# A hybrid mixer layer on one core: the four tiles of the normalised input begin 32, 64, 160 and 192 bytes off the weights' place, mod 256

## The chip, the core and the metric

The kernel runs on one core of a Trainium2 chip. The metric is the device time of one execution in microseconds (us); of several runs the median counts. Engines are named as the profile names them: PE is TensorE (matmuls), PEld its weight loads, DVE is VectorE, ACT ScalarE, POOL GpSimd and SP the engine that issues most transfers. SBUF is the on-chip memory of 128 partitions from which TensorE reads both operands; a tile has the same address in each partition. "Place" means below: the first byte of an operand in its partition, mod 256.

## What is computed

One layer of a decoder trunk over 512 tokens of width 1024, in float32:

```
u = rms_norm(h, norm_mix_pre);  proj = u @ w_in           # 1024 -> 10 slots of 256, 4 gates of 1024
y_a..y_d = four token mixers of the slots                 # width 256 each
branch_out[k] = y_k @ w_branch[k]
merged = sum_k sigmoid(gate_k) * branch_out[k]
h = h + rms_norm(merged @ w_out, norm_mix_post)
u = rms_norm(h, norm_mlp_pre)
h = h + rms_norm(square(relu(u @ w_up)) @ w_down, norm_mlp_post)
```

## The kernel before

TensorE works on float32r operands. To keep float32's precision each operand is split into a high and a low part (hi, lo), and each product is made of three matmuls in `mm3` (lines 238 to 240): hi x hi, hi x lo, lo x hi. Every matmul has a weight load of its own (its first operand, 128 x 128, 512 bytes per partition) and streams its second operand, nearly always 512 columns, 2048 bytes per partition.

The input, multiplied by the gain of the norm, stands transposed in four tiles: `uh[0]`, `uh[1]` (high parts) and `ul[0]`, `ul[1]` (low parts), each 128 x 4 x 512; tile 0 has the contraction steps k = 0 to 3, tile 1 k = 4 to 7. `U(uh, k)` picks 512 columns of it. They are filled at the start (`xhi`, `xlo`, lines 264 to 271) and used until the last gate:

- L323: the first two slots, 96 matmuls, interleaved with the arrival of the data;
- `slot_mm`: the other slots but one and all gates, by `mm3`, weights from `whi` and `wlo`, streams from `uh` and `ul`, into banks `mm` or `sm`. Of three matmuls the first streams uh with whi, the second (L239) ul with whi, the third (L240) uh with wlo, as the profile names them;
- the slot c_i, where the roles are exchanged: pieces of `uh` and `ul` are the weights and 256 columns of the w tiles are streamed (96 matmuls, named `mm<-whi,uh` and the like).

In between stand small float32 matmuls of the mixers (L612, L698, L721 and others), two matmuls that spread the norm's factors over the partitions (L369 and L370, streams from a tile named t, weights a tile of ones) and the branch projections (streams `yhi`, `ylo`).

Behind them come the output projection, its norm, and the MLP. The MLP's input takes the same four buffers of pool `up` again, as `u2h` and `u2l`; the results of its up part stand in banks `ub`, those of its down part in `db`.

Places: a pool lays its buffers one behind the other. All pools that hold matmul operands of 512 columns have buffers whose size is a multiple of 256 bytes, but the pool of tiles named t, whose buffers are of 4224 bytes. So in the program before the weights and the streams `uh`, `ul`, `u2h`, `u2l`, `yhi`, `ylo` all have place 0, and the buffers of t have place 0 and 128 by turns; the one that L369 and L370 stream has 128.

Which instruction stands where on an engine is set by the order in the code and by a scheduler; the order is the same in both programs.

Of the kernel before, what the change touches and what calls it, by code (L numbers as in the profile page):

```python
# [9 lines left out]
F32R = mybir.dt.float32r  # L10
# [5 lines left out]
P = 128  # L16
T = 512
# [32 lines left out]
def tile_hybrid_trunk(ctx: ExitStack, tc: tile.TileContext, x0, xT, xn, wts, dn, par, bd, cst, msk, gains, out):  # L50
# [4 lines left out]
    up = ctx.enter_context(tc.tile_pool(name="up", bufs=4))  # L55
# [17 lines left out]
    def nm(s):  # L73
        cnt[0] += 1
        return f"{s}_{cnt[0]}"
# [90 lines left out]
    def split(hi, lo, src, pin=False):  # L166
        a_ = act.activation(hi, src, AF.Copy)  # L167
        d_ = dve.tensor_tensor(lo, src, hi.bitcast(F32), ALU.subtract)  # L168
        if pin:
            K(a_)  # L170
            K(d_)
# [79 lines left out]
            dve.tensor_tensor(t, t, h, ALU.mult)  # L251
            dve.scalar_tensor_tensor(y, t, 1.5, y, ALU.add, ALU.mult)

    uh = [up.tile([P, 4, T], F32R, tag="u", name=nm("uh")) for _ in range(2)]
    ul = [up.tile([P, 4, T], F32R, tag="u", name=nm("ul")) for _ in range(2)]

    def U(lst, k, a=0, b=T):
        return lst[k // 4][:, k % 4, a:b]
# [180 lines left out]
    o, _ = PAR["corr"]  # L439
# [387 lines left out]
    for ku in range(4):  # L827
        wh, wl = unit()
        for kk in range(2):
            k = 2 * ku + kk  # L830
# [71 lines left out]
    u2h = [None, None]  # L902
    u2l = [None, None]
# [9 lines left out]

    def put(t, j, tv):
        if u2h[j] is None:
            u2h[j] = up.tile([P, 4, T], F32R, tag="u", name=nm("u2h"))
            u2l[j] = up.tile([P, 4, T], F32R, tag="u", name=nm("u2l"))
        split(u2h[j][:, :, t * P : t * P + P], u2l[j][:, :, t * P : t * P + P], tv)

    for t in range(NT):  # L920
# [5 lines left out]
    for j in range(2):  # L926
        put(0, j, tb0[j])

    def mid():
        tb1 = trans(1, mm_bank)  # L930
        for j in range(2):
            put(1, j, tb1[j])
# [53 lines left out]
    for h in range(2):  # L986
        for s in range(2):
            us[s, h] = unit()
            up_mm(bks[s], us[s, h], h, 0, 256)
            if (s, h) in ((1, 0), (0, 1)):  # L990
                t = 2 if h == 0 else 3
                tb = dn_bank()
                for k in range(NK):
                    pe.transpose(tb[:, k // 4, (k % 4) * P : (k % 4) * P + P], u2[t][:, k * P : k * P + P], ident)
                for j in range(2):
                    put(t, j, tb[:, j].rearrange("p (k t) -> p k t", k=4))
# [267 lines left out]
```

## Time and profile before

| | |
|---|---|
| time, median of 3 runs | 748.35 us (748.03 to 748.45) |
| the profiled execution's own time | 748.08 us |
| its span, first to last instruction | 746.3 us |
| PE busy | 735.8 us (99%), 3506 records |
| PEld busy | 620.0 us (83%) |
| DVE, ACT, POOL busy | 535.6 (72%), 312.9 (42%), 6.8 us (1%) |
| TensorE's granted clock, mean | 0.997 of full speed |

A matmul's record is longer than the distance to the next matmul's start, since matmuls are pipelined; records therefore overlap, and busy time is their union. A weight load's record lies beside the matmul before its own. The chain of waits, unlike the records, gives each matmul only the time until the next.

### The profile page before, as it was taken

To read this page: it belongs to the slowest core of one execution; us is meant where nothing else is said; L and a number is where in the kernel's file an instruction comes from. 1 tells how busy PE (TensorE), PEld (TensorE's weight loads), DVE (VectorE), ACT (ScalarE), POOL (GpSimd) and SP (SyncE) were. 2 spreads that over 40 slices of the span, in tenths; PEclk is the share of its full clock that TensorE was granted. 3 is DMA by queue.
4 is the path that set the end of the run, shared out by engine and by line. 5 is a ranking of instruction groups with operands and counts; after the bars stand their busy time and mean duration, and the time that the engine had idled before them with its cause. 6 is when DMAs were issued, how large, how long until landed. Compare 5 with 4: busy or idle time off the path is not lost.

```text
span 746.3 us, 8881 instructions
## 1 busy us (share of the span) xinstructions
PE 735.8 (99%) x3506; PEld 620.0 (83%) x3506; DVE 535.6 (72%) x776; ACT 312.9 (42%) x404; POOL 6.8 (1%) x11
## 2 busy tenths in 40 slices
PE   9999999999999999999999999999999999999995
PEld 7888988888888888888888988888888888888884
DVE  6798347559997476654748785787879685977786
ACT  6434122336324322332444575644445452636232
POOL 1100000000000000000000000000000000000000
PEclk9999999999999999999999999999999999999998
DMA  9634232222222253323332705042423324040312
GB/s 326 244 117 138 96 101 88 83 85 85 94 82 79 85 217 105 102 85 112 113 113 87 296 15 187 38 149 77 141 84 113 113 78 148 0 141 29 132 66 85
DMA packets 22761, 84.59 MB, mean 113 GB/s; under 512 B 2624, under 2 KB 3520, under 8 KB 20928
## 3 DMA queue, kind: packets, MB, share of 16 engines
q1 hardware_dynamic: 22288, 83.74, 32.7%
q8 instruction: 27, 0.44, 0.2%
q10 hardware_dynamic: 432, 0.29, 0.1%
q14 instruction: 14, 0.11, 0.1%
HBM read 79.83 MB, written 4.19 MB: 113 GB/s over the span
## 4 chain that ended last, share of the span: by engine, by line
PE 97%; DVE 1%; DMA 0%; issue 0%; ACT 0%; DVEq 0%
PE mm L238 14%; PE mm L239 14%; PE mm L240 14%; PE ub L239 8%; PE ub L240 8%; PE ub L238 8%; PE db L240 6%; PE db L239 6%; PE db L238 6%; PE mm L323 3%; PE sm L612 2%; PE sm L239 2%; PE sm L238 2%; PE sm L240 2%; PE db L1121 1%; PE db L1120 1%
## 5 line engine op out<-in xcount | busy, mean ns | idle before, releaser
L167 ACT ACTIVATE whi<-raw 128x1024 fp32r<-128x1024 f32 x98 | 103.6, 1060 | 237.4 <-PE mm L239 110.3
L168 DVE TENSOR_TENSOR wlo<-raw,whi 128x1024 fp32r<-128x1024 f32 x98 | 119.5, 1222 | 75.7 <-ACT whi L167 75.5
L240 PE MATMUL mm<-uh,wlo 128*128 128x512 f32 x352 | 137.4, 390 | 0.0
L239 PE MATMUL mm<-ul,whi 128*128 128x512 f32 x352 | 137.3, 390 | 0.0
L238 PE MATMUL mm<-uh,whi 128*128 128x512 f32 x352 | 137.0, 391 | 0.0
L238 PE MATMUL ub<-u2h,whi 128*128 128x512 f32 (+1 forms) x288 | 105.4, 366 | 0.0
L239 PE MATMUL ub<-u2l,whi 128*128 128x512 f32 (+1 forms) x288 | 105.4, 366 | 0.0
L240 PE MATMUL ub<-u2h,wlo 128*128 128x512 f32 (+1 forms) x288 | 105.3, 366 | 0.0
L240 PEld LDWEIGHTS mm<-uh,wlo 128*128 128x128 f32 x352 | 66.1, 188 | 13.7
L238 PEld LDWEIGHTS mm<-uh,whi 128*128 128x128 f32 x352 | 66.2, 188 | 13.4
L239 PEld LDWEIGHTS mm<-ul,whi 128*128 128x128 f32 x352 | 66.1, 188 | 13.4
L240 PE MATMUL db<-fhi,alo 128*128 128x512 f32 x196 | 76.4, 390 | 0.0
L239 PE MATMUL db<-flo,ahi 128*128 128x512 f32 x196 | 76.4, 390 | 0.0
L238 PE MATMUL db<-fhi,ahi 128*128 128x512 f32 x196 | 76.3, 390 | 0.0
L239 PEld LDWEIGHTS ub<-u2l,whi 128*128 128x128 f32 x288 | 54.4, 189 | 8.8
L238 PEld LDWEIGHTS ub<-u2h,whi 128*128 128x128 f32 x288 | 54.3, 189 | 8.7
L240 PEld LDWEIGHTS ub<-u2h,wlo 128*128 128x128 f32 x288 | 54.3, 189 | 8.6
L167 ACT ACTIVATE fhi<-x 128x1024 fp32r<-128x1024 f32 x28 | 29.6, 1059 | 41.0 <-PE db L240 26.6
L1051 DVE TENSOR_TENSOR rows<-rows,db 128x1024 f32<-128x1024 f32 x24 | 29.3, 1219 | 21.9 <-PE db L240 21.8
L239 PEld LDWEIGHTS db<-flo,ahi 128*128 128x128 f32 x196 | 36.8, 188 | 7.7
L238 PEld LDWEIGHTS db<-fhi,ahi 128*128 128x128 f32 x196 | 36.8, 188 | 7.6
L240 PEld LDWEIGHTS db<-fhi,alo 128*128 128x128 f32 x196 | 36.8, 188 | 7.6
(308 smaller groups left out, 1099.5 us busy)
## 6 DMA issues: line engine op xcount, KB each, us to landing
raw<-in_wts_dram SPq DMA_DIRECT2D x102, 512.0 KB, 3.5
ab<-in_dn_dram SPq DMA_DIRECT2D x14, 1024.0 KB, 5.0
t<-in_xn_dram SPq DMA_DIRECT2D x8, 512.0 KB, 7.4
h1d<-t SPq DMA_DIRECT2D x4, 512.0 KB, 2.6
hr<-h1d SPq DMA_DIRECT2D x2, 1024.0 KB, 6.9
xt<-in_xt_dram SPq DMA_DIRECT2D x7, 256.0 KB, 5.7
out_dram<-mg SPq DMA_DIRECT2D x3, 512.0 KB, 2.6
t<-in_gains_dram SPq DMA_DIRECT2D x2, 512.0 KB, 5.8
```

Source lines behind the costliest of these rows:

```text
L167: a_ = act.activation(hi, src, AF.Copy)
L168: d_ = dve.tensor_tensor(lo, src, hi.bitcast(F32), ALU.subtract)
L238: pe.matmul(ps, lh, rh, start=first, stop=False)
L239: pe.matmul(ps, lh, rl, start=False, stop=False)
L240: pe.matmul(ps, ll, rh, start=False, stop=last)
L323: pe.matmul(fb[s_][c], fw[pair[s_]][wi][:, o_ : o_ + P], U(us_, k), start=first and k == 0, stop=last and k == NK - 1)
L612: pe.matmul(bk[ct][:, cs].rearrange("s (h n b) -> s h n b", h=2, b=B), kk_[:, ct, cs], qo, start=True, stop=True)
L1051: dve.tensor_tensor(macc[p], macc[p], ps, ALU.add)
L1120: K(pe.matmul(ps, hh, wl[:, a:b], start=False, stop=False))
L1121: K(pe.matmul(ps, hl, wh[:, a:b], start=False, stop=j == GF - 1))
```

## The change

The four buffers of pool `up` become 64 elements (256 bytes) longer, and a view of 4 x 512 columns begins in them at an element that is given: 8, 16, 40 and 48 elements, which are 32, 64, 160 and 192 bytes. All other tiles keep their place mod 256, those behind the pool in memory move by 1024 bytes. For the MLP's tiles in the same buffers the given element is 0. The same instructions stand in the same order on every engine; behind line 253 line numbers are higher by four.

```diff
-    uh = [up.tile([P, 4, T], F32R, tag="u", name=nm("uh")) for _ in range(2)]
-    ul = [up.tile([P, 4, T], F32R, tag="u", name=nm("ul")) for _ in range(2)]
+    def u_tile(name, shift):
+        t = up.tile([P, 4 * T + 64], F32R, tag="u", name=nm(name))
+        return t[:, shift : shift + 4 * T].rearrange("p (k t) -> p k t", k=4)
+
+    uh = [u_tile("uh", 8), u_tile("uh", 16)]
+    ul = [u_tile("ul", 40), u_tile("ul", 48)]
...
-            u2h[j] = up.tile([P, 4, T], F32R, tag="u", name=nm("u2h"))
-            u2l[j] = up.tile([P, 4, T], F32R, tag="u", name=nm("u2l"))
+            u2h[j] = u_tile("u2h", 0)
+            u2l[j] = u_tile("u2l", 0)
```

## Rows read from the trace of the kernel before

**Rows 1.** The page: busy us (share) and count; the chain that ended last, by engine
```profile
PE 735.8 (99%) x3506; PEld 620.0 (83%) x3506; DVE 535.6 (72%) x776; ACT 312.9 (42%) x404; POOL 6.8 (1%) x11
...
PE 97%; DVE 1%; DMA 0%; issue 0%; ACT 0%; DVEq 0%
```

**Rows 2.** Stretches: us, then busy us and records of each engine, PEclk, DMA
```profile
292.00:356.00 64.00, 64.00 (x284) 53.06 (x283) 33.63 (x42) 20.56 (x26) 0.00 (x0) 1.00 0.30 96
440.00:500.00 60.00, 60.00 (x266) 49.75 (x265) 42.12 (x46) 34.89 (x40) 0.00 (x0) 1.00 0.34 114
```

**Rows 3.** Groups of matmuls by line and shape: count, busy us, mean ns, idle before
```profile
L240 PE MATMUL mm<-uh,wlo 128*128 128x512 f32 x352 | 137.4, 390 | 0.0
L239 PE MATMUL mm<-ul,whi 128*128 128x512 f32 x352 | 137.3, 390 | 0.0
L238 PE MATMUL mm<-uh,whi 128*128 128x512 f32 x352 | 137.0, 391 | 0.0
...
L323 PE MATMUL mm<-ul,whi 128*128 128x512 f32 x32 | 9.2, 389 | 0.0
L239 PE MATMUL mm<-wlo,uh 128*128 128x256 f32 x32 | 9.1, 283 | 0.0
...
L238 PE MATMUL sm<-uh,whi 128*128 128x512 f32 x16 | 6.2, 390 | 0.0
```

**Rows 4.** Single lines, whole span: records' shortest, median, longest ns; first and last start
```profile
L238 PE MATMUL mm<-uh,whi x352: 387/390/477, 38.0 to 353.1; 128*128 128x512 f32 x176
L239 PE MATMUL mm<-ul,whi x352: 388/390/477, 38.2 to 353.3; 128*128 128x512 f32 x176
L240 PE MATMUL mm<-uh,wlo x352: 387/390/478, 38.4 to 353.6; 128*128 128x512 f32 x176
```

**Rows 5.** The same view of the two matmuls that stream place 128
```profile
L369 PE MATMUL sm<-t,ones x1: 396/396/396, 32.3 to 32.3; 128*128 128x512 f32 x1
L370 PE MATMUL sm<-t,ones x1: 396/396/396, 33.2 to 33.2; 128*128 128x512 f32 x1
```

**Rows 6.** Timeline of PE around them: start us, length us, line, tiles, count
```profile
31.84 0.39 PE L240 MATMUL sm<-uh,wlo 128*128 128x512 f32 x1
32.06 0.39 PE L238 MATMUL sm<-uh,whi 128*128 128x512 f32 x1
32.29 0.40 PE L369 MATMUL sm<-t,ones 128*128 128x512 f32 x1
32.52 0.39 PE L239 MATMUL sm<-ul,whi 128*128 128x512 f32 x1
32.75 0.39 PE L238 MATMUL sm<-uh,whi 128*128 128x512 f32 x1
32.98 0.39 PE L239 MATMUL sm<-ul,whi 128*128 128x512 f32 x1
33.20 0.40 PE L370 MATMUL sm<-t,ones 128*128 128x512 f32 x1
33.44 0.62 PE L240 MATMUL sm<-uh,wlo 128*128 128x512 f32 x2
```

**Rows 7.** Single lines as in 4, only from 260.5 to 264 us, behind L698
```profile
L240 PE MATMUL mm<-uh,wlo x4: 389/394/397, 261.3 to 263.4; 128*128 128x512 f32 x4
...
L238 PE MATMUL mm<-uh,whi x5: 390/398/476, 260.8 to 263.6; 128*128 128x512 f32 x5
...
L239 PE MATMUL mm<-ul,whi x5: 388/389/390, 261.1 to 263.9; 128*128 128x512 f32 x5
```

**Rows 8.** The chain of waits in order of time: start us, us, what
```profile
266.53 0.89 PE sm L721 x8
```

**Rows 9.** Writers of the tiles, to 27 us, and the chain's first matmuls
```profile
L271 DVE SCALAR_TENSOR_TENSOR ul<-xt,x0t,uh 128x512 fp32r<-128x512 f32 x7 | 5.0, 749 | 0.8 <-ACT uh L266 0.6
L266 ACT ACTIVATE uh<-xt,x0t 128x512 fp32r<-128x512 f32 x7 | 4.8, 718 | 0.6 <-DMA xt<-in_xt_dram 0.6
L264 DVE TENSOR_SCALAR uh<-x0t 128x512 fp32r<-128x512 f32 x1 | 0.5, 487 | 3.0 <-DMA x0t<-in_x_dram 3.0
...
4.62 22.17 PE mm L323 x96
```

## The prediction

> **What bounds the kernel now.** Read the busy times and the chain of waits first: TensorE is busy for 99% of the span and the chain that ended last is TensorE for 97% of it [rows 1]. Nothing that another engine does is late; the time is the number of matmuls times the distance from one start to the next. So the second view is the one by stretches. From 292 to 356 us, in the gates, 284 matmul records touch 64 us; one record lasts 0.39 us, so starts between 291.61 and 356 count, and 64.39 / 284 = 226.7 ns. From 440 to 500 us, in the MLP, 60.39 / 266 = 227.0 ns. The clock is granted in full, 1.00, in both [rows 2]. 512 columns at 2.4 GHz would take 213.3 ns, so each matmul of 512 columns costs some 13.4 ns more than its columns, everywhere. Each one has its own weight load, which runs beside the matmul before it.
>
> Third, the records of single matmuls. A record's length is not the distance between starts, but it goes with it: in the two long trains it is 390 ns (median) where the distance is 227. I therefore read differences of records as differences of distance. In the slots and gates the median is 390 for all three kinds and the shortest is 387 [rows 4].
>
> **What the change touches.** It removes and adds no instruction, and no engine's order changes. What is different is where four tiles begin. In the built program the weights begin at 0 mod 256, and so did the four input tiles; now uh[0], uh[1], ul[0], ul[1] begin 32, 64, 160 and 192 bytes off. The pool grows by 4 x 256 bytes, so all tiles behind it move by 1 KiB and keep their place mod 256. The MLP's u2h and u2l are put back at 0.
>
> Matmuls that stream these tiles: L238, L239 and L240 with 352 each in one bank set, L323 three groups of 32, and three groups of 16 in the other bank set [rows 3]: 3 x (352 + 32 + 16) = 1200. Of three, two stream uh and one ul, and half of the k steps take tile 0: 400 at 32, 400 at 64, 200 at 160, 200 at 192. Besides, 96 matmuls of 256 columns (three groups of 32) load the input as weights and stream w [rows 3].
>
> The writers: 15 of the 16 operations that fill the tiles at the start are of 0.7 us, and one of 0.5 [rows 9]. They write the same elements to other places. TensorE walked through the 96 matmuls beside them in 22.17 us, 231 ns each with the late first one included [rows 9], so they are not late now. Should each grow by a tenth, 16 x 0.07 = 1.1 us would be spread over two engines inside these 22 us: I take nothing, and keep 0.5 us for the range.
>
> **Does the place matter at all?** The trace has few rows with another place, but two are clean. L369 and L370 stream a tile that begins at 128 mod 256, against weights at 0, in the midst of a train of matmuls with place 0. Both records are 396 ns [rows 5], where the median is 390 [rows 4]. The starts agree: from 31.84 to 33.44 seven distances make 1600 ns, five at 226.7 are 1133.5, so 466.5 is left for the two, 233 each, with some 5 ns of rounding [rows 6]. So a matmul 128 bytes off costs 6 to 7 ns more; I take 6.5.
>
> A second look says that the 13.4 ns are no fixed fee either. After a group of narrow matmuls (L698, before 261 us) the same tiles at the same place give records of 389 to 397 and 390 to 398 for some matmuls and 388 to 390 for others, until the train has settled [rows 7] (476 there is the first one, which waited for its weights). What a matmul loses depends on how its stream and the weight load lie to each other. That is the same thing that the change alters.
>
> On what the four offsets cost I have no row, only the two ends: nothing at 0, 6.5 at 128. My theory: both streams read the same memory, in an order that repeats every 256 bytes, and the faster one loses time behind the slower. The matmul reads 2048 bytes in at least 213 ns, 9.6 bytes per ns. A load reads 512 bytes; narrow matmuls, which cannot go faster than their loads, follow at 0.89 / 8 = 111 ns [rows 8], so some 4.6 bytes per ns. The stream gains 5 bytes per ns on the load. If it begins just ahead it needs a whole lap to meet the load from behind, and is then held back for a short rest only; if it begins further ahead it meets it earlier and is held back longer. By this the loss grows with the lead, evenly until it falls back near 256: 6.5 / 128 = 0.051 ns per byte. An estimate, from the two ends:
>
> 32: 1.6 ns x 400 = 0.65 us. 64: 3.25 x 400 = 1.3 us. 160: 8.1 x 200 = 1.6 us. 192: 9.75 x 200 = 1.95 us. Sum 5.5 us.
>
> For the 96 narrow ones the roles are exchanged: the stream leads by 224 and 192 (32 each) or 96 and 64 (16 each); 11.4, 9.75, 4.9 and 3.25 ns make 0.8 us, or nothing where 224 has fallen back and the load finishes anyway. I take the middle, 0.4.
>
> Bounds from both sides: the shortest record in the stage is 387, the longest ordinary one 398 [rows 4, 7]. Were all 1200 at the one or the other, the sum would be -3 x 1200 = -3.6 us or +8 x 1200 = +9.6 us.
>
> What else is late then? Nothing else can become the bound: the other engines get more time per matmul. There is also no cover for the loss, since the chain is TensorE without a gap.
>
> A sentence of the Trainium skill speaks against all this. The page "TensorE: Matmul & The Clock Gate", section "Step-by-step: what each phase is for", says that streaming operand and weight load have two independent read ports, so that loading the next weights takes no read bandwidth from the running matmul; by that rule the place does nothing and the time stays. The same page of the Trainium skill gives N/2.4 + 2.5 ns in "Back-to-back issue gap", 215.8 for 512 columns; the trace has 227, and 396 against 390 in rows that differ in place, so here the trace does not bear it out.
>
> **Sum.** The profiled execution took 748.1 us (span 746.3, and 1.8 around it), 0.3 under the median of the runs. 748.1 + 5.5 + 0.4 = 754.0, and against the median 754.3.
>
> **Rivals.**
> 1. Any place off 256 costs the same, 6.5 ns, for instance because a read that begins within such a block touches one block more. 1200 x 6.5 = 7.8 us, with 0.4 from the narrow ones 756.5. For it: the only place measured says just this much. Against: the unsettled trains change cost without changing place.
> 2. The loss goes by the distance to the nearest multiple of 256: 32, 64, 96, 64 bytes. 0.65 + 1.3 + 200 x 4.9 + 200 x 3.25 ns = 3.6 us, with the narrow ones 752.2. Nothing in the rows separates it from my forecast but the picture of the faster stream catching up.
> 3. Nothing happens: the 6 ns of L369 and L370 belong to something else in these two (their weights are a tile of ones), not to the place. 748.3. For it: two rows are few. (The Trainium skill's rule on the two ports, above, would have it so.)
> 4. Faster. Place 0 is itself a bad one and 128 a worse; off it the streams meet less. The place is in the stream of each of the 1200, the price up to -13.4 ns if all above the columns went, 16 us and 732; by the shortest record -3 ns, 744.7. It decides as soon as the mean over 32, 64, 160 and 192 (weights 2, 2, 1, 1) is below 0, for instance 32 and 64 at -3 and the far two at +3: -2.4 + 1.2 = -1.2 us, 747.1. For it: 13.4 ns stand there unexplained. Against it: 128 is dearer, and none of the unsettled ones goes below 387.
> 5. The kernel doesn't do what it says, since the MLP's tiles share the buffers: excluded, since they are given 0 again in the code.
>
> **How the numbers follow.** Forecast 0.35, rival 1 0.20, rival 2 0.11, rival 3 0.15, rival 4 0.19. A measurement of this kernel can tell some 0.2%, 1.5 us, from no change. Slower by more is then 0.66 (the forecast and rivals 1 and 2), faster by more 0.17 (rival 4 but for its mildest cases), within 0.17. The range reaches to rival 3 and to the mild half of rival 4, 746.0, and at the top to 9.6 us and 0.8 for the narrow ones with the writers' half us and a slope a little steeper, 760.0; it leaves out some 0.10 below and 0.06 above.
>
> **What would show it.** The MLP's stretches must stay at 227 ns, records 390 for u2h and u2l; if they move, the place of these tiles is not the cause. In the gates L239 (ul, 160 and 192) should have records of 398 to 400 and L238 and L240 (uh, 32 and 64) of 391 to 394: two pairs of lines that part say that the lead counts. All three at 396 is rival 1; L239 at 394 and uh at 391 to 393 rival 2; all at 390 rival 3; records under 387 rival 4. The forecast is wrong if the gates' distance is not between 229 and 234 ns.

## The result, and the profile after

The changed kernel took 754.19 us (median of 4 runs, 753.85 to 754.62) against 748.40 us; the ratio is 1.0074 (1.0060 to 1.0088). The profiled execution took 753.97 us with a span of 752.2, 5.9 us more than before.

The page of the changed kernel: busy us with shares, and the chain that ended last, by engine.

```profile
PE 741.6 (99%) x3506; PEld 619.2 (82%) x3506; DVE 536.1 (71%) x776; ACT 312.8 (42%) x404; POOL 6.6 (1%) x11
...
PE 97%; DVE 1%; DMA 0%; issue 0%; ACT 0%; DVEq 0%
```

Against [rows 1] PE has grown by 5.8 us, with the same number of records; no other engine has changed by more than 0.8 us. The chain is TensorE as before.

Where the time lies can be read from first and last starts. The view of single lines, changed kernel: shortest, median and longest record in ns, first and last start in us.

```profile
L238 PE MATMUL mm<-uh,whi x352: 389/393/484, 38.6 to 358.9; 128*128 128x512 f32 x176
L238 PE MATMUL ub<-u2h,whi x288: 277/389/396, 410.4 to 714.7; 128*128 128x512 f32 x112, 128*128 128x256 f32 x32
...
L239 PE MATMUL mm<-ul,whi x352: 388/393/485, 38.8 to 359.1; 128*128 128x512 f32 x176
...
L240 PE MATMUL mm<-uh,wlo x352: 388/397/482, 39.1 to 359.4; 128*128 128x512 f32 x176
```

The first matmul of this group starts at 38.6 instead of 38.0, so 0.6 us were lost in the first slots. From the first to the last it is 320.3 us, where [rows 4] have 315.1: 5.2 more. In the MLP it is 304.3 us (410.4 to 714.7). The same line in the kernel before:

```profile
L238 PE MATMUL ub<-u2h,whi x288: 278/389/397, 404.5 to 708.8; 128*128 128x512 f32 x112, 128*128 128x256 f32 x32
```

That is 304.3 us as well: the MLP, whose tiles kept their place, lost nothing. The two stretches of [rows 2] in the changed kernel:

```profile
292.00:356.00 64.00, 64.00 (x283) 52.08 (x282) 35.56 (x45) 21.47 (x27) 0.00 (x0) 1.00 0.32 98
440.00:500.00 60.00, 60.00 (x267) 49.67 (x266) 44.17 (x50) 36.32 (x41) 0.00 (x0) 1.00 0.29 97
```

The clock is granted in full in both. The gates have nearly as many records in 64 us as before, but the changed kernel is by then some 5 us behind, and this stretch holds eight of the small matmuls (L746) that the stretch of the kernel before does not hold; a stretch at a fixed time is a poor measure here, and the starts above are the better one.

The remaining terms of the sum, by rows that answer to [rows 3, 9]: the matmuls that load the input as weights, and the writers of the tiles.

```profile
L239 PE MATMUL mm<-wlo,uh 128*128 128x256 f32 x32 | 9.0, 280 | 0.0
```

```profile
L275 DVE SCALAR_TENSOR_TENSOR ul<-xt,x0t,uh 128x512 fp32r<-128x512 f32 x7 | 5.1, 750 | 0.5 <-ACT uh L270 0.3
L270 ACT ACTIVATE uh<-xt,x0t 128x512 fp32r<-128x512 f32 x7 | 4.8, 719 | 0.7 <-DMA xt<-in_xt_dram 0.6
```

The narrow matmuls became a little faster (280 ns against 283), and the writers took what they took.

The distances from a matmul's start to the next one's in the trace, over all matmuls of 512 columns that stream an input tile (longer gaps beside small matmuls left out), sorted by the place of the tile streamed by the first matmul of the two, before and after:

```
place of the stream   matmuls   distance before   after, mean   lost in all
 32 (uh[0])             400         226.9 ns        232.8 ns      2.4 us
 64 (uh[1])             400         226.9           230.7         1.5
160 (ul[0])             200         226.9           234.2         1.5
192 (ul[1])             200         226.9           229.9         0.6
narrow, input loaded     96         119.7           117.7        -0.2
```

Together 5.8 us: nearly the whole loss (the span grew by 5.9) is in these matmuls. The forecast sum was 5.5 + 0.4, but its parts are not these, which the experiments take up.

Single rows of this table must be read with care. Places 32 and 160 stand next to each other in every train (a "train" is a row of matmuls that follow each other without a gap), and 64 and 192 likewise, and a distance belongs to two matmuls. Put down to the second of the two, 160 and 192 come to 231.5 and 231.3 ns. What does not hang on this is the pair: 233.2 ns for tile 0 (32 and 160), 230.5 for tile 1 (64 and 192).

### The profile page after: what moved, and what is told of

Its sections match the earlier page's. It is cut to its first block, busy times and chain, and to the rows that moved or that the text cites. A ratio compares the mean times of both kernels' runs of the same rounds, so it can differ in the third digit from the quotient of the medians.

```text
span 752.2 us, 8881 instructions
## 1 busy us (share of the span) xinstructions
PE 741.6 (99%) x3506; PEld 619.2 (82%) x3506; DVE 536.1 (71%) x776; ACT 312.8 (42%) x404; POOL 6.6 (1%) x11
## 4 chain that ended last, share of the span: by engine, by line
PE 97%; DVE 1%; DMA 0%; issue 0%; ACT 0%; DVEq 0%
PE mm L240 14%; PE mm L239 14%; PE mm L238 14%; PE ub L239 8%; PE ub L238 8%; PE ub L240 8%; PE db L239 6%; PE db L238 6%; PE db L240 6%; PE mm L327 3%; PE sm L616 2%; PE sm L240 2%; PE sm L238 2%; PE sm L239 2%; PE db L1123 1%; PE db L1124 1%
## 5 line engine op out<-in xcount | busy, mean ns | idle before, releaser
L240 PE MATMUL mm<-uh,wlo 128*128 128x512 f32 x352 | 139.1, 395 | 0.0
L239 PE MATMUL mm<-ul,whi 128*128 128x512 f32 x352 | 138.7, 394 | 0.0
L238 PE MATMUL mm<-uh,whi 128*128 128x512 f32 x352 | 138.3, 395 | 0.0
L238 PE MATMUL ub<-u2h,whi 128*128 128x512 f32 (+1 forms) x288 | 105.2, 366 | 0.0
L239 PE MATMUL ub<-u2l,whi 128*128 128x512 f32 (+1 forms) x288 | 105.2, 365 | 0.0
L240 PE MATMUL ub<-u2h,wlo 128*128 128x512 f32 (+1 forms) x288 | 105.2, 365 | 0.0
L239 PEld LDWEIGHTS mm<-ul,whi 128*128 128x128 f32 x352 | 66.1, 188 | 15.5
L240 PEld LDWEIGHTS mm<-uh,wlo 128*128 128x128 f32 x352 | 66.1, 188 | 15.1
L238 PEld LDWEIGHTS mm<-uh,whi 128*128 128x128 f32 x352 | 66.0, 188 | 15.2
L238 PE MATMUL db<-fhi,ahi 128*128 128x512 f32 x196 | 76.3, 389 | 0.0
L239 PE MATMUL db<-flo,ahi 128*128 128x512 f32 x196 | 76.3, 389 | 0.0
L240 PE MATMUL db<-fhi,alo 128*128 128x512 f32 x196 | 76.2, 389 | 0.0
L240 PEld LDWEIGHTS ub<-u2h,wlo 128*128 128x128 f32 x288 | 54.3, 189 | 8.7
L238 PEld LDWEIGHTS ub<-u2h,whi 128*128 128x128 f32 x288 | 54.2, 189 | 8.8
L239 PEld LDWEIGHTS ub<-u2l,whi 128*128 128x128 f32 x288 | 54.3, 189 | 8.7
L238 PEld LDWEIGHTS db<-fhi,ahi 128*128 128x128 f32 x196 | 36.8, 188 | 7.9 <-DVE macc L1055 0.2
L240 PEld LDWEIGHTS db<-fhi,alo 128*128 128x128 f32 x196 | 36.8, 188 | 7.6
L239 PEld LDWEIGHTS db<-flo,ahi 128*128 128x128 f32 x196 | 36.8, 188 | 7.6
```

Of the source, the lines that this page charges most:

```text
L238: pe.matmul(ps, lh, rh, start=first, stop=False)
L239: pe.matmul(ps, lh, rl, start=False, stop=False)
L240: pe.matmul(ps, ll, rh, start=False, stop=last)
```

## Experiments

All kernels below compute the same thing with the same instructions in the same order; only begins of tiles differ. The expectations of all32 and ul32 name lines L242 to L244; the matmuls of `mm3` stand at lines 238 to 240 in every kernel, since the changed lines come behind them.

### One operand off, both off, a whole lap off

all32, all128 and all256 give all four tiles the same place:

```diff
-    uh = [u_tile("uh", 8), u_tile("uh", 16)]
-    ul = [u_tile("ul", 40), u_tile("ul", 48)]
+    uh = [u_tile("uh", 8), u_tile("uh", 8)]      # all128: 32, all256: 64
+    ul = [u_tile("ul", 8), u_tile("ul", 8)]      # all128: 32, all256: 64
```

all32: 

> All four input tiles 32 bytes off the weights' place, nothing else changed. Theory of the step (32 off the weights costs what it showed in the changed kernel: 394 to 395 ns a record in L242, L244): all 1200 matmuls lose 6 ns, +7.2 us, 755.5. Theory of the lead (the loss grows evenly with the distance ahead, 0.051 ns a byte): 1.6 ns each, +1.9 us, 750.3. Theory of the alternation (what costs is that neighbours in the train stand at different places, and a train of one place settles): records of 390, 748.4.

all128: 

> All four input tiles 128 bytes off. Step and lead agree here: 6 to 7 ns each as in L369 and L370 of the kernel before, +7.2 to +8.4 us, 755.5 to 756.8. Alternation: records of 390, 748.4.

all256: 

> All four input tiles 256 bytes off, which is the weights' place again mod 256 but not mod 512. If the memory's order repeats every 256 bytes (or a part of them): records of 390, 748.4. If it repeats every 512 or more: slower, by the lead 13 ns each, +15.6 us, 764.

mem32 is the kernel before with one change:

```diff
-    cp.tile([P, 40], F32, name="pad")
+    cp.tile([P, 48], F32, name="pad")
```

mem32: 

> The kernel before, with an unused tile 32 bytes longer, so that every buffer behind it, weights and streams alike, begins 32 bytes later: the absolute place is 32, the place of the streams off the weights 0. If the place of the stream alone counts: 6 ns on some 2950 matmuls of 512 columns, +17.7 us, 766. If only the place of the two to each other counts: records of 390, 748.4.

Measured: all32 756.29 us, ratio 1.0104 (1.0087 to 1.0121); all128 755.70, 1.0095 (1.0080 to 1.0110); all256 748.64, 0.9997 (0.9988 to 1.0007); mem32 748.64, 1.0000 (0.9990 to 1.0009). The kernel before stood at 748.74 beside them. Single lines of all32:

```profile
L238 PE MATMUL mm<-uh,whi x352: 392/396/484, 39.7 to 361.6; 128*128 128x512 f32 x176
...
L239 PE MATMUL mm<-ul,whi x352: 390/395/483, 39.9 to 361.9; 128*128 128x512 f32 x176
...
L240 PE MATMUL mm<-uh,wlo x352: 389/395/493, 40.1 to 362.1; 128*128 128x512 f32 x176
```

of all128:

```profile
L238 PE MATMUL mm<-uh,whi x352: 387/393/479, 39.2 to 360.5; 128*128 128x512 f32 x176
```

of all256:

```profile
L238 PE MATMUL mm<-uh,whi x352: 387/389/477, 38.4 to 353.5; 128*128 128x512 f32 x176
```

and of mem32, a gate line and one of the MLP:

```profile
L238 PE MATMUL mm<-uh,whi x352: 388/390/477, 38.6 to 353.7; 128*128 128x512 f32 x176
L238 PE MATMUL ub<-u2h,whi x288: 278/389/396, 405.1 to 709.4; 128*128 128x512 f32 x112, 128*128 128x256 f32 x32
```

From first to last start: 321.9 us at 32, 321.3 at 128, 315.1 at 256 and in mem32, as before. Three things follow. In mem32 every stream begins 32 bytes later, as in all32, but its weights do too, and nothing is lost: only the place of the operands to each other counts. 256 is as good as 0, while 128 is not: the order repeats after 256 bytes and not after 128, and it is not the moved or longer buffer that costs. And 32 bytes cost as much as 128 (mean distances 233.3 and 232.7 ns against 226.9), where the theory of the lead wanted 1.6 ns and 6.5: it fails at its near end. The theory of the alternation, that a train of one place settles at 227 ns whatever the place, is refuted too.

### The other places

The same edit with 16 elements (all64), 24 (all96), 40 (all160), 48 (all192), 56 (all224) and 4 (all16), for instance:

```diff
-    uh = [u_tile("uh", 8), u_tile("uh", 16)]
-    ul = [u_tile("ul", 40), u_tile("ul", 48)]
+    uh = [u_tile("uh", 56), u_tile("uh", 56)]
+    ul = [u_tile("ul", 56), u_tile("ul", 56)]
```

all64: 

> All four input tiles 64 bytes off. Theory of classes (odd multiples of 32 cost 6 to 7 ns, odd multiples of 64 some 3.5, as 64 and 192 did in the changed kernel): records of 392 to 393, +4.3 us, 752.9. Theory of the lead: 3.25 ns, +3.9 us, 752.5. Theory of settling (at place 0 a train falls into a fixed rhythm of 227 ns, at any other it does not, and costs what an unsettled train costs at place 0): 4 to 6 ns, +4.8 to +7.2 us.

all96: 

> All four input tiles 96 bytes off. Classes: as at 32, 6.5 ns, +7.8 us, 756.3. Lead: 4.9 ns, +5.9 us, 754.5. Settling: 4 to 6 ns, +4.8 to +7.2 us, unless 96 has a rhythm of its own.

all192: 

> All four input tiles 192 bytes off. Classes: as at 64, +4.3 us, 752.9, and the two traces read alike. Lead: 9.75 ns, +11.7 us, 760.3. Settling: 4 to 6 ns, +4.8 to +7.2 us.

all224: 

> All four input tiles 224 bytes off, that is 32 short of the weights' place. Classes: as at 32, 6.5 ns, +7.8 us, 756.3. Lead: 11.4 ns, +13.7 us, 762, or, where the lead has fallen back before the end of the lap, below 227 ns a matmul and under 748.4. Settling: 4 to 6 ns, +4.8 to +7.2 us.

all160: 

> All four input tiles 160 bytes off. The places 32, 96, 192 and 224 gave a mean distance of 233.3 ns, 128 gave 232.7 and 64 gave 229.1; the theory of classes wants 233.3 here, +7.9 us, 756.3. Lead (already refuted at 224): 8.1 ns, 758.0.

all16: 

> All four input tiles 16 bytes off. If what counts are units of 32 bytes or more in which both operands are read, a stream that begins within the unit still starts in step: 227 to 229 ns, 748.4 to 750.8. If any distance counts: 233 ns, 755.5 to 756.3.

Measured: all64 751.88 us, 1.0049 (1.0029 to 1.0069); all96 756.93, 1.0116 (1.0087 to 1.0146); all192 756.04, 1.0105 (1.0075 to 1.0134); all224 755.78, 1.0101 (1.0072 to 1.0130); all160 756.86, 1.0113 (1.0093 to 1.0133); all16 754.01, 1.0075 (1.0055 to 1.0095); medians of four runs for all64, of two for the others. The kernel before stood at 748.29 beside the first four, at 748.43 beside the last two and beside the kernels of the two sections that follow. One line of each, first all64:

```profile
L238 PE MATMUL mm<-uh,whi x352: 387/392/480, 38.9 to 356.4; 128*128 128x512 f32 x176
```

all160:

```profile
L238 PE MATMUL mm<-uh,whi x352: 392/397/479, 39.1 to 362.0; 128*128 128x512 f32 x176
```

all192:

```profile
L238 PE MATMUL mm<-uh,whi x352: 392/394/483, 39.0 to 360.9; 128*128 128x512 f32 x176
```

all224:

```profile
L238 PE MATMUL mm<-uh,whi x352: 392/396/482, 39.1 to 360.8; 128*128 128x512 f32 x176
```

all16:

```profile
L238 PE MATMUL mm<-uh,whi x352: 390/394/482, 38.8 to 359.0; 128*128 128x512 f32 x176
```

and two of all96, whose lines part:

```profile
L238 PE MATMUL mm<-uh,whi x352: 388/392/484, 39.7 to 361.8; 128*128 128x512 f32 x176
...
L240 PE MATMUL mm<-uh,wlo x352: 390/399/484, 40.1 to 362.3; 128*128 128x512 f32 x176
```

In the last both lines stream the same tiles, L238 with records of 392 and L240 of 399. So the loss of a matmul is not set by its place alone. The distances in the trace show more. One after the other within one long train of gate matmuls, in ns, and the mean over all slots and gates:

```
kernel   place   distances one after the other, in the train      mean
before     0     227 226 227 227 226 227 ...                      226.9
all16     16     235 230 227 235 | 235 230 227 234 | ...          231.6
all32     32     231 235 233 234 | 231 235 234 234 | ...          233.3
all64     64     232 226 229 | 232 226 229 | ...                  229.1
all96     96     231 231 238 | 231 231 238 | ...                  233.4
all128   128     237 230 237 229 | 237 230 237 229 | ...          232.7
all160   160     233 232 237 238 231 234 235 | ...                234.2
all192   192     233 234 233 | 233 234 233 | ...                  233.3
all224   224     232 235 | 231 235 | 232 235 | ...                233.3
all256   256     227 227 226 227 227 226 ...                      226.9
```

Every place has a rhythm, a pattern of distances that repeats, into which its train falls. In these trains it is one matmul long at 0 and 192, two at 128 and 224, three at 64 and 96, four at 16 and 32, seven at 160. (Starts are read to 1 ns, so 227 226 227 is an even 226.7 and 233 234 233 an even 233.3. In other trains 128 has a rhythm of seven and 192 one of two.) In all96 the rhythm has the length of the three lines, and the long distance of it, 237 ns or more, falls to L240 for 190 of 366 matmuls and to L238 for 54 of 363; hence the medians of 399 and 392.

Of the theories: the lead (11.4 ns at 224, 9.75 at 192) is refuted; both cost 6.4 ns, and its other reading, that 224 is faster than 0, is refuted with it. Classes (odd multiples of 64 cheap) fails at 192, which costs 6.4 where 64 costs 2.2. Units of 32 bytes or more fails at 16, which costs 4.7. Settling, as it was put, is half right: the other places do not stay unsettled, they settle into slower rhythms, and 64 into a fairly cheap one. None of these places is better than 0.

### Is the loss the matmul's own?

ul32 puts the high parts at 0 and the low parts at 32:

```diff
+    uh = [u_tile("uh", 0), u_tile("uh", 0)]
+    ul = [u_tile("ul", 8), u_tile("ul", 8)]
```

ul32: 

> Only the low parts 32 bytes off, the high parts at the weights' place: of three matmuls in a row one stands at 32 and two at 0. Theory of places that add up (each matmul has the cost of its own place): 400 lose 6.7 ns, as all1200 did at 32, +2.7 us, 751.2; records of 390 in L242 and L244, 396 in L243. Theory of settling (the fixed rhythm of 227 ns is a property of an undisturbed train; one matmul in three at another place keeps throwing it out): the two at place 0 lose some 4 ns too, +2.7 + 800 x 4 = +5.9 us, 754.4; records above 390 in all three lines.

Measured: 754.69 us, 1.0084 (1.0069 to 1.0099). Single lines of ul32:

```profile
L238 PE MATMUL mm<-uh,whi x352: 389/395/477, 38.7 to 359.2; 128*128 128x512 f32 x176
...
L239 PE MATMUL mm<-ul,whi x352: 391/395/483, 38.9 to 359.5; 128*128 128x512 f32 x176
...
L240 PE MATMUL mm<-uh,wlo x352: 388/393/477, 39.2 to 359.7; 128*128 128x512 f32 x176
```

L238 and L240 stream tiles at place 0 and still have medians of 395 and 393 in place of 390. In the trains the distances go 236 232 232, or 237 226 231: the matmul at 32 and what it does to its neighbours together cost 13 to 20 ns in each three. Had each matmul only the cost of its own place, 400 x 6.4 = 2.6 us would be lost; from first to last start it is 320.5 us, 5.4 more than before, and 6.3 us in time. One stream out of three off the place costs four fifths of what three cost (all32: 6.8 us from first to last start, 7.6 us in time).

### The same off place in the MLP

mlp32 leaves the slots and gates at 0:

```diff
+    uh = [u_tile("uh", 0), u_tile("uh", 0)]
+    ul = [u_tile("ul", 0), u_tile("ul", 0)]
...
-            u2h[j] = u_tile("u2h", 0)
-            u2l[j] = u_tile("u2l", 0)
+            u2h[j] = u_tile("u2h", 8)
+            u2l[j] = u_tile("u2l", 8)
```

mlp32: 

> The slots and gates as in the kernel before, all at place 0; the MLP's input tiles 32 bytes off the weights instead. If the rule is one of the two operands and not of the stage: the 672 matmuls of 512 columns of the up part lose 6.7 ns each, +4.5 us, the 192 of 256 columns gain up to 3 or lose up to 6.7 ns (-0.6 to +1.3), 752.3 to 754.2, the gates back at records of 390. If it belongs to the slots and gates: 748.5.

Measured: 752.89 us, 1.0059 (1.0042 to 1.0076). Single lines, then the two shapes of one MLP line, of mlp32:

```profile
L238 PE MATMUL mm<-uh,whi x352: 387/389/476, 38.1 to 353.3; 128*128 128x512 f32 x176
L238 PE MATMUL ub<-u2h,whi x288: 277/394/399, 404.7 to 713.8; 128*128 128x512 f32 x112, 128*128 128x256 f32 x32
```

```profile
L240 PE MATMUL ub<-u2h,wlo 128*128 128x512 f32 x224 | 88.6, 395 | 0.0
L240 PE MATMUL ub<-u2h,wlo 128*128 128x256 f32 x64 | 17.8, 279 | 0.0
```

In the kernel before the last two were:

```profile
L240 PE MATMUL ub<-u2h,wlo 128*128 128x512 f32 x224 | 87.3, 390 | 0.0
L240 PE MATMUL ub<-u2h,wlo 128*128 128x256 f32 x64 | 18.1, 283 | 0.0
```

The gates are back at 389 and 315.2 us, and the MLP's line runs 309.1 us where it ran 304.3, 4.8 more. In the trace this is a sum of three: 672 matmuls x 6.7 ns (226.7 to 233.4) are 4.5 us lost; the 192 of 256 columns gain 3 ns each (120.7 to 117.6), 0.6 us; and the 672 matmuls of the down part, whose tiles kept their place, lose 0.9 us (226.7 to 228.1 ns on average): they come in 33 groups behind matmuls of the up part, and the first eight of a group take 228 to 233 ns, from the ninth on 226.7. The time grew by 4.5 us. The effect belongs to the operands, not to the stage.

## Why the prediction was right, and where its working was not

The forecast was 754.3 us, the measured median is 754.19; sign, size and stage are right. Step by step:

1. **TensorE alone sets the time, and nothing covers a longer matmul.** Right: the chain is TensorE for 97% as before, and the matmuls' 5.8 us are the change but for 0.1 us of the span.
2. **The place counts, read from L369 and L370 and from the trains behind narrow matmuls.** Right, and the runs make it firm: mem32 and all256 at 748.6, all others above, 751.9 to 756.9. Rival 3, nothing happens, is refuted. Here the Trainium skill's sentence in "TensorE: Matmul & The Clock Gate", section "Step-by-step: what each phase is for", that loading the next weights takes nothing from the running matmul, does not account for what the traces show: the same streams beside the same loads take 226.9 ns at place 0 and 233.3 at 32.
3. **6.5 ns at 128.** A little high: 128 alone costs 5.8 ns (232.7 - 226.9). The 6.5 came from two lone matmuls in a train of place 0, which is not the same thing as a train at 128.
4. **The loss grows evenly with the lead.** This step failed. It wanted 1.6, 3.25, 8.1 and 9.75 ns for 32, 64, 160 and 192; alone, in all32, all64, all160 and all192, these places lose 6.4, 2.2, 7.3 and 6.4, in no order of the distance, and in the changed kernel, by the table above, 5.9, 3.8, 7.3 and 3.0. The picture under the step was not shown either: that a load reads 4.6 bytes per ns was taken from the distances of L721's narrow matmuls [rows 8], which show how often these follow each other and not how long a load reads. The sum agrees because the 800 matmuls of the near places were put 2.0 us too low, the 400 of the far ones 1.5 us and the narrow ones (step 5) 0.6 us too high. That agreement is luck, and the check that the prediction itself named says so: L239 was to have records of 398 to 400 and has 393, and L240, put at 391 to 394, has 397.
5. **The 96 narrow ones lose 0.4 us.** Wrong in sign: they gained 0.2, the case that the bound left open only as "nothing".
6. **Writers and MLP unchanged.** Right, 750 and 719 ns against 749 and 718, and 304.3 us against 304.3.

Of the rivals, 1 (any place off costs the same) has the better picture of the sizes: six places alone cost 5.8 to 7.3 ns each, though 16 and 64 only 4.7 and 2.2. But its reason, a read that touches one block more, is refuted by mem32, where the streams begin where they do in all32 and nothing is lost. Rival 2 (the distance to the nearest multiple) fails at 32 and 224, which cost as much as 96, or 6.4 ns where it wanted 1.6. Rival 4 (place 0 is a bad one) is refuted for 512 columns by eight other places, and holds, by up to 3 ns, for 256.

What stays open is the mechanism. The trains fall into steady rhythms that differ from place to place, and what a matmul loses depends on the matmuls before it; that is shown. That the partner is the weight load beside the matmul, the load for the next one, is the natural reading, since all streams of all32 stand at one place and only the weights at another. One row of mem32 points the same way. The tile `ones`, the weights of L369 and L370, stands in the code before the lengthened pad and so keeps its place there, while streams and all other weights of 512-column matmuls move by 32 bytes. The matmul beside which `ones` is loaded for L369 is an L238 in an undisturbed train, its own weights at the place of its stream. Its record in the kernel before and in mem32:

```profile
L238 PE MATMUL sm<-uh,whi x1: 389/389/389, 32.1 to 32.1; 128*128 128x512 f32 x1
```

```profile
L238 PE MATMUL sm<-uh,whi x1: 397/397/397, 32.6 to 32.6; 128*128 128x512 f32 x1
```

It takes 235 ns to the next start where it took 227, behind matmuls of 226 and 227 in both, and of what stands around it only the place of the load beside it has changed. It is one matmul, so this supports the reading and does not prove it. The loads' own records do not grow: those of L238 in the gates, from 300 to 340 us, in the kernel before and in all32:

```profile
L238 PEld LDWEIGHTS mm<-uh,whi 128*128 128x128 f32 x45 | 8.5, 188 | 1.8
```

```profile
L238 PEld LDWEIGHTS mm<-uh,whi 128*128 128x128 f32 x42 | 7.9, 188 | 1.9
```

No run here has a matmul without a load beside it, and what in the memory gives way was not tried.

## What to carry to other kernels

Where a train of float32r matmuls of 512 columns has a weight load beside each of them, put streams and weights at the same place mod 256; it was worth 2.2 to 7.3 ns of 227 a matmul here. Buffers whose sizes are multiples of 256 bytes keep the place by themselves; buffers of another size, such as the 4224-byte tiles here, do not. The mean distance between starts in a long train tells whether it holds, 226.7 ns here against 229 to 234. For 256 columns the runs showed no loss off the place, and mostly a small gain. And a sum that comes out right does not prove its terms: check the term by the rows that it names.

## What the runs showed of the hardware that was not expected

- The loss is a property of the train. One stream out of three at place 32 makes the two others, at place 0, slower by 3 to 5 ns (ul32: 231.9 and 230.5 ns for L238 and L240). Behind a change of place or a group of small matmuls it takes up to some eight matmuls until the train has its rhythm again (the down part's groups in mlp32; in the kernel before, a train behind small matmuls goes 234 236 227 233 231 and then 226 and 227).
- The rhythms add up to whole multiples of 6.67 ns, within 0.1 ns when averaged over a train: 226.7 = 34 x 6.67 (0, one matmul), 233.3 = 35 x 6.67 (192, one), 467 = 70 x 6.67 (128 and 224, two), 687 = 103 x 6.67 (64, three), 700 = 105 x 6.67 (96, three), 927 = 139 x 6.67 (16, four), 933 = 140 x 6.67 (32, four), 1640 = 246 x 6.67 (160, seven). At the prediction's estimate of 9.6 bytes per ns a stream reads 64 bytes per partition in 6.67 ns; whether that is the reason was not tried.
- For 256 columns it is the other way round: off the weights' place the narrow matmuls that load the input took 117 to 119 ns, where they took 120 at the same place; only at 160 was nothing gained.
